# A second feed-forward product in seven block products, with the norms shared between VectorE and GpSimd

## The chip, the cores and the metric

One core of one Trainium2 chip runs the whole program. The metric is the device time in microseconds (us): the median of three timed runs is 3547.95 us, the runs lie between 3546.67 and 3548.14 us. All numbers of the trace come from one profiled execution, which took 3548.3 us; its recorded span, from the first to the last instruction, is 3546.4 us.

## The reference

Two layers work on 1056 tokens (1024 of a prompt, 32 of a sample group) of 1024 features. Only the second half of a layer matters here:

```python
x = layer_norm(ALPHA * x + mix @ w_out, ln1_g, ln1_b)
h = square(relu(x @ w_ff_up))                    # 1024 -> 4096 features
x = layer_norm(ALPHA * x + h @ w_ff_down, ln2_g, ln2_b)   # 4096 -> 1024

def layer_norm(x, g, b):
    mu = mean(x); var = mean(square(x - mu))
    return (x - mu) * rsqrt(var + 1e-5) * g + b
```

Ahead of it stand the input product, sliding-window attention and an RWKV-7 recurrence. All values are float32.

## The kernel before

**Layout.** Features lie on the 128 partitions, tokens in the columns. The tokens form three chunks: 0 and 1 of 384 columns, 2 of 288. A float32 product is made of three matmuls: each operand is split into a high part (a cast on ScalarE, L287 for data, L236 for weights) and the remainder as a low part (a subtraction on VectorE, L288 and L237), and high x high, high x low and low x high are summed in a PSUM bank (`gemm_parts`, `products`, `mmul` L206). A weight tile is 128 x 1024 (512 KB, loaded at L223), a block of features 128 x 384 (192 KB) or 128 x 288.

**Feed-forward, first product (`ff`).** The first four feature tiles are made chunk by chunk (`up`). The other 28 go by pairs (`pair_up`): for chunks 0 and 1, seven products stand in for the eight of a 2 x 2 block product; chunk 2 is done directly. Each result is passed through relu (ScalarE), squared (mostly on GpSimd, L1367) and stored in `d_h` in device memory, one transfer per tile and chunk.

**Second product.** 32 feature tiles are taken in eight groups of four. `features(g)` loads the 12 blocks of the next group (L1461) and splits them while the present group is multiplied. For each of 8 output tiles and 3 chunks, `down` sums 12 matmuls in one PSUM bank, and VectorE adds the bank to an accumulator in SBUF (L1472). The accumulators start as the residual, loaded from `d_x` (L1507).

**Norms.** `layer_norm` takes the mean from a product with ones, subtracts it (VectorE, L339), squares (ScalarE, L341), sums the squares (VectorE and GpSimd, L348), forms the reciprocal root by a Newton iteration on tiny tiles (VectorE, L298 to L302, L357), spreads it with a matmul, multiplies (L364), adds the bias and splits (ScalarE L369, VectorE L370). It is a generator in three parts: `book` puts these at given TensorE times (`LN_TIMES`, `LN1_TIMES`) among the matmuls that follow, and the order on TensorE is as written. In the last group the second product runs chunk by chunk, so chunks 0 and 1 are normed among the matmuls of the next chunk; chunk 2 comes last by itself. The other engines' order is set by a list scheduler; each engine, and SyncE's DMA queue, works strictly in its order.

**Buffers.** Blocks and splits live in slots (`Slots`): 16 "outer" ones per chunk (`x`), 20 "inner" ones per chunk (`i`), handed out and given back in program order.

## Time and profile before

| | |
|---|---|
| median of the runs | 3547.95 us |
| profiled execution, its span | 3548.3 us, 3546.4 us |
| TensorE busy | 3425.7 us, 97% |
| VectorE, ScalarE, GpSimd busy | 61%, 33%, 22% |
| chain that ended last | TensorE 83%, VectorE 6%, DMA 2% |
| granted TensorE clock, mean | 0.978 |

In layer 0 the branch products and the first norm end near 1062 us, the pairs of the first product run from about 1100 to 1385 us, the second product from there to about 1720 us, and layer 1 begins among its last norm. The second layer's second product ends at 3516 us, and the last chunk's norm follows alone. Busy time of an engine is an average over stages; what a stage waits for is in the view of waits, and what engines and DMA do in a stretch is in the table of windows.

### The profile page before, as it was taken

To read this page: it belongs to the slowest core of one execution; us is meant where nothing else is said; L and a number is where in the kernel's file an instruction comes from. 1 tells how busy PE (TensorE), PEld (TensorE's weight loads), DVE (VectorE), ACT (ScalarE), POOL (GpSimd) and SP (SyncE) were. 2 spreads that over 40 slices of the span, in tenths; PEclk is the share of its full clock that TensorE was granted. 3 is DMA by queue.
4 is the path that set the end of the run, shared out by engine and by line. 5 is a ranking of instruction groups with operands and counts; after the bars stand their busy time and mean duration, and the time that the engine had idled before them with its cause. 6 is when DMAs were issued, how large, how long until landed. Compare 5 with 4: busy or idle time off the path is not lost.

```text
span 3546.4 us, 65145 instructions
## 1 busy us (share of the span) xinstructions
PE 3425.7 (97%) x24950; PEld 3174.9 (90%) x24950; DVE 2153.1 (61%) x5492; ACT 1174.6 (33%) x2653; POOL 790.9 (22%) x1134
## 2 busy tenths in 40 slices
PE   8999999998989999999999999999999899999997
PEld 8688888888979999999897888888899799999997
DVE  4746778756476555444657467778473855554445
ACT  4654322222153333221237443222221533331112
POOL 2223423211122331000232234232101322310002
PEclk9999999999989999999999999999999999999998
DMA  5123323326213336232031333232251233362211
GB/s 169 62 87 115 86 77 85 83 67 202 66 64 118 110 99 197 93 97 77 13 89 49 100 102 91 79 84 82 100 176 48 90 111 110 107 197 87 90 47 50
DMA packets 282359, 342.08 MB, mean 96 GB/s; under 512 B 111168, under 2 KB 244832, under 8 KB 282016
## 3 DMA queue, kind: packets, MB, share of 16 engines
q1 hardware_dynamic: 253152, 297.84, 28.0%
q10 hardware_dynamic: 27360, 35.57, 2.8%
q8 instruction: 196, 3.21, 0.4%
q0 software_dynamic: 1536, 4.52, 0.3%
q14 instruction: 115, 0.94, 0.1%
HBM read 232.24 MB, written 102.21 MB: 94 GB/s over the span
## 4 chain that ended last, share of the span: by engine, by line
PE 83%; DVE 6%; DMA 2%; issue 1%; ACT 1%; POOL 1%; SPq 0%; ACTq 0%; DVEq 0%; POOLq 0%
PE mm L206 35%; PE b L206 25%; PE c L206 21%; PE b L210 1%; PE c L210 0%; PE b L793 0%; DVE pd L1019 0%; DVE i L364 0%; DVE x L1294 0%; DVE x L370 0%; DMA i<-d_x 0%; DMA x<-d_h 0%; DVE Xt L1021 0%; DMA i<-d_yr 0%; DMA d_g<-gs 0%
## 5 line engine op out<-in xcount | busy, mean ns | idle before, releaser
L206 PE MATMUL mm<-x,w 128*128 128x384 f32 (+1 forms) x6630 | 1320.9, 335 | 17.6 <-ACT x L287 8.5
L206 PEld LDWEIGHTS mm<-x,w 128*128 128x128 f32 x6630 | 1077.6, 190 | 72.5 <-issue 12.5
L236 ACT CAST w<-raw 128x1024 fp32r<-128x1024 f32 x260 | 273.0, 1050 | 568.1 <-PE b L206 364.3
L206 PE MATMUL b<-x,w 128*128 128x384 f32 (+1 forms) x1958 | 457.4, 320 | 0.8 <-DVE x L288 0.8
L206 PE MATMUL mm<-i,w 128*128 128x384 f32 (+1 forms) x2034 | 421.5, 328 | 19.0 <-ACT i L287 14.4
L237 DVE TENSOR_TENSOR w<-raw,w 128x1024 fp32r<-128x1024 f32 x260 | 321.4, 1236 | 176.6 <-ACT w L236 176.0
L206 PE MATMUL c<-i,w 128*128 128x384 f32 (+1 forms) x2080 | 426.8, 326 | 1.2 <-DVE i L1309 1.2
L206 PE MATMUL b<-i,w 128*128 128x384 f32 (+1 forms) x1570 | 391.6, 324 | 5.4 <-ACT i L287 5.4
L206 PEld LDWEIGHTS mm<-i,w 128*128 128x128 f32 x2034 | 347.3, 192 | 21.4 <-ACT i L287 14.6
L206 PEld LDWEIGHTS c<-i,w 128*128 128x128 f32 x2080 | 353.9, 191 | 3.7 <-DVE i L1309 1.8
L206 PEld LDWEIGHTS b<-x,w 128*128 128x128 f32 x1958 | 334.2, 188 | 1.5 <-DVE x L288 1.5
L206 PE MATMUL c<-x,w 128*128 128x384 f32 (+1 forms) x1424 | 311.9, 323 | 0.0
L206 PEld LDWEIGHTS b<-i,w 128*128 128x128 f32 x1570 | 276.4, 188 | 6.0 <-ACT i L287 6.0
L206 PEld LDWEIGHTS c<-x,w 128*128 128x128 f32 x1424 | 242.4, 190 | 0.5 <-DVE x L288 0.5
L1367 POOL TENSOR_TENSOR x<-x 128x384 f32<-128x384 f32 x112 | 114.5, 1023 | 365.2 <-ACT x L1366 319.9
L313 POOL TENSOR_TENSOR i<-i,i 128x384 f32<-128x384 f32 (+1 forms) x36 | 34.7, 963 | 686.3 <-DVE i L1472 680.1
L1472 DVE TENSOR_TENSOR i<-i,b 128x384 f32<-128x384 f32 x144 | 74.8, 520 | 144.2 <-PE b L206 143.7
L821 POOL TENSOR_TENSOR z<-z,gs 128x384 f32<-128x384 f32 (+1 forms) x84 | 80.2, 954 | 287.0 <-issue 184.4
L1366 ACT ACTIVATE x<-x 128x384 f32<-128x384 f32 x112 | 58.6, 523 | 246.1 <-DVE x L1434 153.6
L1100 POOL COPY sav<-vt 64x128 f32<-64x128 f32 x128 | 42.7, 334 | 331.6 <-PE c L206 300.2
L1127 DVE COPY sav<-c 64x128 f32<-64x128 f32 x128 | 36.9, 288 | 126.2 <-PE c L206 125.2
L287 ACT CAST x<-x 128x384 fp32r<-128x384 f32 (+1 forms) x126 | 60.5, 497 | 152.2 <-DMA x<-d_h 108.4
(349 smaller groups left out, 4974.2 us busy)
## 6 DMA issues: line engine op xcount, KB each, us to landing
raw<-in_w_in_dram SPq DMA_DIRECT2D x72, 512.0 KB
raw<-in_w_up_dram SPq DMA_DIRECT2D x64, 512.0 KB
raw<-in_w_down_dram SPq DMA_DIRECT2D x64, 512.0 KB
x<-d_h SPq DMA_DIRECT2D x128, 192.0 KB
d_h<-x SPq DMA_DIRECT2D x112, 192.0 KB
d_g<-gs ACTq DMA_DIRECT2D x64, 192.0 KB
i<-d_g SPq DMA_DIRECT2D x64, 192.0 KB
d_z<-z ACTq DMA_DIRECT2D x52, 192.0 KB
```

The source lines that it names most:

```text
L206: return self.nc.tensor.matmul(out, lhsT=lhsT, rhs=rhs, start=start, stop=stop)
L210: self.nc.tensor.transpose(out, x, ident)
L236: nc.scalar.copy(wf[:, 0, :], raw)
L237: self.weng.tensor_tensor(wf[:, 1, :], raw, wf[:, 0, :].bitcast(F32), op=ALU.subtract)
L287: self.nc.scalar.copy(hi, src)
L313: eng.tensor_tensor(sums[c].f, a, acc[k][c].f, op=ALU.add)
L821: nc.gpsimd.tensor_tensor(out[:, :n], out[:, :n], prev[:, :n], op=ALU.add)
L1100: nc.gpsimd.tensor_copy(sav[Kk, :], vt[Kk, k // 2, :])
L1127: nc.vector.tensor_copy(sav[B, :], sa[B, 0:128])
L1366: nc.scalar.activation(out=z.f, in_=z.f, func=AF.Relu)
L1367: P(z.f, z.f, z.f, op=ALU.mult)
L1472: nc.vector.tensor_tensor(a, a, p[:, :n], op=ALU.add)
```

## The change

The second product becomes seven block products over all 32 feature tiles, in the order 1, 2, 5, 4, 6, 7, 3. Feature tiles are taken in pairs and chunks 0 and 1 as the two column halves of a 2 x 2 block product. Each product has 8 jobs, and a job has one weight tile and two 128 x 384 blocks: 24 matmuls into four banks, which are kept over all 8 jobs. In products 1, 2, 5 and 4 a job also carries 24 matmuls on two 128 x 288 blocks of chunk 2, which is done directly. The combinations of squared features are formed once, in the first product: `quad` makes three more differences on GpSimd and one on VectorE per pair and stores seven blocks (`d_t`), `third` makes one for chunk 2 and stores three (`d_c`). The combinations of weights are made on GpSimd job by job (`weights`): one 128 x 1024 sum or difference per job in products 5, 6, 7 and 3. Blocks are now streamed: `prepare` loads and splits those of the job after next. What lands in the banks goes to the outputs in `done`, with a running sum per chunk for the norm (`total`).

In the norms, two of eight subtractions, three of eight multiplications and the three low parts behind them, and three of six sums of squares are on GpSimd; PSUM is copied by ScalarE first for these. The second norm's order is chunk 2 (booked at product 6), chunk 0 (at product 3), chunk 1 last; the next layer's attention takes the chunks in the order 0, 2, 1. The accumulators of chunks 0 and 1 share one set of 20 inner slots.

```diff
         sq = []
+        ms = get()
+        nc.scalar.copy(ms.f, pm[:, :n])
         for k in range(KD):
-            nc.vector.tensor_tensor(a[k], a[k], pm[:, :n], op=ALU.subtract)
+            if k in (1, 3):
+                nc.gpsimd.tensor_tensor(a[k], a[k], ms.f, op=ALU.subtract)
+            else:
+                nc.vector.tensor_tensor(a[k], a[k], pm[:, :n], op=ALU.subtract)
...
             else:
-                eng = (nc.vector, nc.gpsimd)[k % 2]
+                eng = nc.gpsimd if k < 5 else nc.vector
...
             self.mmul(pr[:, o:o + m], lhsT=rb[:, bi, :], rhs=self.ident[:, o - b:o - b + m], start=True, stop=True)
+        rs = get()
+        nc.scalar.copy(rs.f, pr[:, :n])
         for k in range(KD):
-            nc.vector.scalar_tensor_tensor(a[k], a[k], par[:, gcol + k:gcol + k + 1], pr[:, :n],
-                                           op0=ALU.mult, op1=ALU.mult)
-            bk = par[:, bcol + k:bcol + k + 1]
+            bk, gk = par[:, bcol + k:bcol + k + 1], par[:, gcol + k:gcol + k + 1]
+            pool = k in (1, 3, 5)
+            if pool:
+                nc.gpsimd.tensor_tensor(a[k], a[k], rs.f, op=ALU.mult)
+            else:
+                nc.vector.scalar_tensor_tensor(a[k], a[k], gk, pr[:, :n], op0=ALU.mult, op1=ALU.mult)
+            scale = gk if pool else 1.0
             if out is None:
                 hi, lo = [(self.outer if self.outer.free[c] else tmp).get(c, F32R) for _ in range(2)]
-                nc.scalar.activation(out=hi.t, in_=a[k], func=AF.Identity, bias=bk)
-                nc.vector.scalar_tensor_tensor(lo.t, a[k], bk, hi.f, op0=ALU.add, op1=ALU.subtract)
+                nc.scalar.activation(out=hi.t, in_=a[k], func=AF.Identity, bias=bk, scale=scale)
+                if pool:
+                    nc.scalar.activation(out=a[k], in_=a[k], func=AF.Identity, bias=bk, scale=scale)
+                    nc.gpsimd.tensor_tensor(lo.t, a[k], hi.f, op=ALU.subtract)
+                else:
+                    nc.vector.scalar_tensor_tensor(lo.t, a[k], bk, hi.f, op0=ALU.add, op1=ALU.subtract)
                 if keep is None:
                     acc[k].put()
...
+        def quad(k, b11, b12, b21, b22):
+            t1, t2, t4 = [get(0, F32) for _ in range(3)]
+            P(t1.f, b12.f, b11.f, op=ALU.subtract)
+            V(b12.f, b22.f, b12.f, op=ALU.subtract)
+            P(t2.f, b22.f, t1.f, op=ALU.subtract)
+            P(t4.f, t2.f, b21.f, op=ALU.subtract)
+            for t, z in ((1, b11), (5, t1), (7, b12), (3, b22), (6, t2), (2, b21), (4, t4)):
+                store(d_t[t - 1, k], z)
+        def third(k, x1, x2):
+            xd = get(2, F32)
+            P(xd.f, x2.f, x1.f, op=ALU.subtract)
+            for t, z in enumerate((x1, x2, xd)):
+                store(d_c[t, k], z)
...
+    def ff_down(self, l, inner, small, keep):
+        nc, tc, i = self.nc, self.tc, self.i
+        d_x, d_t, d_c = self.d_x[l], self.d_t[l], self.d_c[l]
+        V, P, S = nc.vector.tensor_tensor, nc.gpsimd.tensor_tensor, nc.vector.scalar_tensor_tensor
+        n, n2 = CH[0][1], CH[2][1]
+        acc = [[None] * 3 for _ in range(KD)]
+        sums = [Fixed(keep.tile([128, CH[c][1]], F32, tag=f"sum{c}", name=self.nm("sum"))) for c in range(3)]
+        sk = {}
+        def weights(p, k):
+            raw = lambda q: self.wraw(i["w_down"][l, q, k])
+            if p in (1, 2, 4):
+                return self.wsplit(raw({1: 0, 2: 1, 4: 3}[p]))
+            if p == 5:
+                a, b = raw(2), raw(3)
+                sk[k] = keep.tile([128, 1024], F32, tag=f"s{k}", name=self.nm("sk"))
+                P(sk[k], a, b, op=ALU.add)
+                return self.wsplit(sk[k])
+            if p == 6:
+                P(sk[k], sk[k], raw(0), op=ALU.subtract)
+                return self.wsplit(sk[k])
+            a = raw(3 if p == 7 else 1)
+            P(a, a, sk[k], op=ALU.subtract)
+            return self.wsplit(a)
+        def block(src, c):
+            z = self.outer.get(c)
+            nc.sync.dma_start(out=z.f, in_=src)
+            return self.parts(z, lambda: self.outer.get(c, F32R))
+        def prepare(p, k):
+            x = [block(d_t[p - 1, 2 * k + q], 1) for q in range(2)]
+            t = {1: 0, 2: 1, 5: 0, 4: 2}.get(p)
+            y = [block(d_c[t, 2 * k + q], 2) for q in range(2)] if t is not None else []
+            return weights(p, k), x, y
+        def residual(m, c):
+            acc[m][c] = inner.get(c)
+            nc.sync.dma_start(out=acc[m][c].f, in_=d_x[m, :, CH[c][0]:CH[c][0] + CH[c][1]])
+        def add(e, x, sign=1.0):
+            S(e, e, sign * ALPHA, x, op0=ALU.mult, op1=ALU.add)
+        def total(c, m, first, eng):
+            if first:
+                nc.scalar.copy(sums[c].f, acc[m][c].f)
+            else:
+                eng.tensor_tensor(sums[c].f, sums[c].f, acc[m][c].f, op=ALU.add)
+        def done(p, mp, e, y):
+            m = 2 * mp
+            if p == 1:
+                u[mp] = self.outer.get(0)
+                nc.scalar.copy(u[mp].f, e)
+            elif p == 2:
+                add(acc[m][0].f, e)
+                add(acc[m][2].f, y)
+                P(acc[m][0].f, acc[m][0].f, u[mp].f, op=ALU.add)
+                total(0, m, mp == 0, nc.gpsimd)
+                total(2, m, mp == 0, nc.gpsimd)
+            elif p == 5:
+                add(acc[m][1].f, e)
+                add(acc[m + 1][1].f, e)
+            elif p == 4:
+                add(acc[m + 1][2].f, y)
+                total(2, m + 1, False, nc.vector)
+                add(acc[m + 1][0].f, e, -1.0)
+            elif p == 6:
+                V(u[mp].f, u[mp].f, e, op=ALU.add)
+                P(acc[m][1].f, acc[m][1].f, u[mp].f, op=ALU.add)
+            elif p == 7:
+                V(u[mp].f, u[mp].f, e, op=ALU.add)
+                V(acc[m + 1][0].f, u[mp].f, acc[m + 1][0].f, op=ALU.subtract)
+                total(0, m + 1, False, nc.vector)
+                P(acc[m + 1][1].f, acc[m + 1][1].f, u[mp].f, op=ALU.add)
+                total(1, m + 1, mp == 0, nc.gpsimd)
+                u[mp].put()
+            else:
+                V(acc[m][1].f, acc[m][1].f, e, op=ALU.add)
+                total(1, m, False, nc.vector)
...
+                ends = dict(start=(k == 0 and q == 0), stop=(k == 7 and q == 1))
+                for t, z, nn, ends in ((e, x, n, ends), (y, xc, n2, dict(
+                        start=(p in (1, 5) and k == 0 and q == 0), stop=(p in (2, 4) and k == 7 and q == 1)))):
+                    for mp in range(4 if z else 0):
+                        hi, lo = z[q]
+                        for j, (a, b) in enumerate(((0, hi), (0, lo), (1, hi))):
+                            self.mmul(t[mp][:, :nn], lhsT=w[:, a, 4 * q + mp, :], rhs=b.t, start=ends["start"] and j == 0,
+                                      stop=ends["stop"] and j == 2)
+                            self.due(self.pe_ns)
...
+                if q + 2 < len(jobs):
+                    ready.append(prepare(*jobs[q + 2]))
+                if k == 0:
+                    if p in (1, 5):
+                        y = fours()
+                    e = fours() if p in (6, 3) else [self.ps(self.pb, "b") for _ in range(4)]
+                if (p, k) == (6, 0):
+                    self.book(norm(2), LN2_TIMES)
+                elif (p, k) == (3, 0):
+                    self.book(norm(0), LN2_TIMES)
+                if k == 3:
+                    for mp in range(4):
+                        for m, c in {2: ((0, 0), (0, 2)), 5: ((0, 1), (1, 1)), 4: ((1, 0), (1, 2))}.get(p, ()):
+                            residual(2 * mp + m, c)
+                w, x, xc = ready.popleft()
+                product(p, k, e, y, w, x, xc)
+                for t in x + xc:
+                    for z in t:
+                        z.put()
+                if k == 7:
+                    for mp in range(4):
+                        done(p, mp, e[mp][:, :n], y[mp][:, :n2])
             self.due()
...
```

**SyncE's queue in the second product.** `raw` is a weight load, `x0`/`x1` a block of 384 columns, `x2` one of 288; the digits behind are the slot and two running numbers, and the brackets name what the row waits for. Before, in the third and fourth group:

```order
L1461 DMA x0_13_2916_16300<-d_h0_104 128x384 [waits PE_49]
L1461 DMA x0_1_2990_16740<-d_h0_104 128x384 [waits DMAHW5_49,DVE_49]
L1461 DMA x0_7_2972_16704<-d_h0_104 128x384 [waits DMAHW6_49,DMAHW2_49,DVE_49]
L1461 DMA x0_4_2919_16306<-d_h0_104 128x384 [waits DMAHW7_49,PE_49]
L1461 DMA x2_6_2931_16330<-d_h0_104 128x288 [waits DMAHW0_49,PE_49]
L1461 DMA x2_1_2934_16336<-d_h0_104 128x288 [waits DMAHW1_49,PE_49]
L1461 DMA x0_13_2975_16710<-d_h0_104 128x384 [waits DMAHW4_49,DVE_49]
```

After, in products 6 and 7 of layer 0:

```order
L1572 DMA x1_11_3432_18844<-d_t0_104 128x384 [waits DMAHW6_49,DMAHW4_49,DVE_49]
L1572 DMA x1_5_3437_18880<-d_t0_104 128x384 [waits PE_49]
L240 DMA raw_3505_19163<-in_w_down_dram 128x1024 [waits DMAHW0_49,DVE_49]
L1572 DMA x1_11_3440_18886<-d_t0_104 128x384 [waits DMAHW6_49,DMAHW1_49,DVE_49]
L1572 DMA x1_1_3463_18971<-d_t0_104 128x384 [waits PE_49]
L240 DMA raw_3513_19205<-in_w_down_dram 128x1024 [waits DMAHW3_49,DVE_49,Pool_49]
L1572 DMA x1_11_3466_18977<-d_t0_104 128x384 [waits DMAHW1_49,DVE_49]
L1572 DMA x1_9_3471_19013<-d_t0_104 128x384 [waits DMAHW5_49,PE_49]
L1572 DMA x1_14_3479_19063<-d_t0_104 128x384 [waits PE_49]
```

Before, the group's blocks go through many slots. Now two blocks come per job, and every second one is put into the same slot, `x1_11`, whose row waits for VectorE (the split of the block that lay there); the other waits for TensorE.

**GpSimd in the second product.** Before, nothing stood there between the last squares of the first product and the sums of the norm:

```order
L1367 TENSOR_TENSOR x0_2_2765_15625<-x0_2_2765_15625 128x384 [waits Activation_49]
L1446 TENSOR_TENSOR x2_5_2772_15718<-x2_5_2772_15718 128x288 [waits DMAHW3_49,Activation_49,Pool_49]
L313 TENSOR_TENSOR i0_0_2_3319_18888<-i0_0_8_2773_15722,i0_0_0_2776_15725 128x384 [waits DVE_49]
L313 TENSOR_TENSOR i0_0_2_3319_18888<-i0_0_2_3319_18888,i0_0_1_2779_15728 128x384 [waits DVE_49,Pool_49]
L313 TENSOR_TENSOR i0_0_2_3319_18888<-i0_0_2_3319_18888,i0_0_12_2782_15731 128x384 [waits DVE_49,Pool_49]
```

After, around the end of product 6 in layer 0 (L1567 is a weight difference, L393 and L402 the norm of chunk 2, L1616 a sum of outputs):

```order
L393 TENSOR_TENSOR i0_2_13_3331_18257<-i0_2_13_3331_18257,i0_2_4_3446_18912 128x288
L402 TENSOR_TENSOR x2_3_3450_18921<-i0_2_6_3327_18249,x2_14_3449_18920 128x288 [waits DMAHW5_49,DMAHW4_49,Activation_49]
L1567 TENSOR_TENSOR raw_3513_19205<-raw_3513_19205,sk_3196_17590 128x1024 [waits DMAHW3_49,DVE_49]
L402 TENSOR_TENSOR x2_9_3454_18932<-i0_2_10_3329_18253,x2_15_3453_18931 128x288 [waits PE_49,Activation_49]
L402 TENSOR_TENSOR x2_5_3458_18943<-i0_2_13_3331_18257,x2_1_3457_18942 128x288 [waits PE_49,Activation_49]
L1616 TENSOR_TENSOR i0_0_16_3198_17595<-i0_0_16_3198_17595,x0_15_2994_16639 128x384 [waits DVE_49]
L1616 TENSOR_TENSOR i0_0_14_3200_17599<-i0_0_14_3200_17599,x0_7_2995_16641 128x384 [waits DVE_49]
L1616 TENSOR_TENSOR i0_0_17_3202_17603<-i0_0_17_3202_17603,x0_8_2996_16643 128x384 [waits DVE_49]
L1616 TENSOR_TENSOR i0_0_5_3204_17607<-i0_0_5_3204_17607,x0_9_2997_16645 128x384 [waits DVE_49]
L1567 TENSOR_TENSOR raw_3521_19247<-raw_3521_19247,sk_3220_17687 128x1024 [waits DMAHW0_49,Activation_49]
L1567 TENSOR_TENSOR raw_3529_19289<-raw_3529_19289,sk_3236_17768 128x1024 [waits DMAHW3_49,DVE_49,Activation_49]
L1567 TENSOR_TENSOR raw_3537_19331<-raw_3537_19331,sk_3108_17157 128x1024 [waits DMAHW6_49,DVE_49]
```

The row holds weight differences of 128 x 1024 between the steps of the norm and the sums of outputs; in products 7 and 3 they follow one another.

## Rows read from the trace of the kernel before

**Rows 1.** The page: span, busy time by engine, 40 slices of TensorE and its clock.

```profile
span 3546.4 us, 65145 instructions
...
PE 3425.7 (97%) x24950; PEld 3174.9 (90%) x24950; DVE 2153.1 (61%) x5492; ACT 1174.6 (33%) x2653; POOL 790.9 (22%) x1134
...
PE   8999999998989999999999999999999899999997
...
PEclk9999999999989999999999999999999999999998
```

**Rows 2.** Timeline of TensorE in the second product: start, length, instruction.

```profile
1650.69 0.30 PE L206 MATMUL b<-i,w 128*128 128x288 f32 x1
...
1652.28 0.34 PE L206 MATMUL mm<-x,w 128*128 128x384 f32 x1
...
1654.37 0.33 PE L206 MATMUL b<-x,w 128*128 128x384 f32 x1
```

**Rows 3.** Windows: stretch, its length, busy time by engine, clock, DMA share, GB/s.

```profile
1110.00:1360.00 250.00, 250.00 (x1575) 250.00 (x1574) 130.96 (x177) 81.56 (x132) 75.38 (x72) 1.00 0.34 108
1360.00:1410.00 50.00, 47.12 (x286) 46.18 (x284) 28.92 (x53) 21.59 (x43) 6.87 (x8) 0.97 0.82 261
1410.00:1700.00 290.00, 290.00 (x1817) 290.00 (x1816) 136.22 (x242) 56.72 (x91) 0.00 (x0) 1.00 0.28 86
...
1388.00:1392.00 4.00, 3.83 (x13) 3.31 (x13) 2.98 (x7) 1.59 (x4) 0.14 (x1) 0.57 0.93 296
```

**Rows 4.** Timeline of all engines: block loads and what splits them.

```profile
1567.06 4.86 SPq L1461 DMA_DIRECT2D x<-d_h  x6
...
1569.39 0.51 ACT L287 CAST x<-x 128x384 fp32r<-128x384 f32 x1 [7.91 <-DMA x<-d_h]
1569.94 0.56 DVE L288 TENSOR_TENSOR i<-x,x 128x384 fp32r<-128x384 f32 x1 [1.11 <-ACT x L287]
...
1375.53 3.81 SPq L1461 DMA_DIRECT2D x<-d_h  x7
1380.00 0.51 ACT L287 CAST x<-x 128x384 fp32r<-128x384 f32 x1 [8.94 <-DMA x<-d_h]
```

**Rows 5.** Timeline of VectorE and GpSimd beside each other, 78 to 136 us.

```profile
78.13 5.69 POOL L487 TENSOR_TENSOR qh<-qraw,qh 64x1024 fp32r<-64x1024 f32 x2 [0.63 <-ACT qh L486]
...
79.31 2.28 DVE L237 TENSOR_TENSOR w<-raw,w 128x1024 fp32r<-128x1024 f32 x1
81.51 2.34 DVE L468 TENSOR_SCALAR m<-m 128x2 f32<-128x2 f32 x1
...
86.16 0.16 DVE L468 TENSOR_SCALAR m<-m 128x2 f32<-128x2 f32 x1
...
86.50 1.22 DVE L237 TENSOR_TENSOR w<-raw,w 128x1024 fp32r<-128x1024 f32 x1
...
132.84 2.33 POOL L487 TENSOR_TENSOR qh<-qraw,qh 64x1024 fp32r<-64x1024 f32 x1
```

**Rows 6.** One line's instructions (L313): duration ns minimum/median/maximum over the span.

```profile
L313 POOL TENSOR_TENSOR i<-i,x x36: 803/1014/1108, 936.1 to 2774.9; 128x384 f32<-128x384 f32 x24, 128x288 f32<-128x288 f32 x12
```

**Rows 7.** TensorE's waits, 975 to 1062 us: waited for, total, times, longest.

```profile
PE b L206 <- DVE ln_rb L357: 9.8, 2, 7.4
PE b L206 <- DVE i L313: 5.3, 1, 5.3
```

**Rows 8.** TensorE's waits, 1360 to 1700 us.

```profile
PE b L206 <- ACT i L287: 2.6, 1, 2.6
```

**Rows 9.** TensorE's waits, 1700 to 1800 us.

```profile
PE b L206 <- DVE i L313: 5.1, 1, 5.1
PE b L206 <- DVE ln_rb L357: 2.4, 2, 1.3
```

**Rows 10.** Timeline of the end of the program.

```profile
3518.27 0.72 PE L206 MATMUL b<-i,ones 128*128 128x288 f32 x2
...
3539.14 3.57 ACT L376 ACTIVATE i<-i,par 128x288 f32<-128x288 f32 x8 [13.12 <-DVE i L364]
```

More of the change, by code (lines that the diff above doesn't have):

```diff
@@ L97, in put, with __init__ @@
         self.pool.free[self.c].append(self.j)
+class Fixed:
+    def __init__(self, t):
+        self.f = t
+    def put(self):
+        pass
 class Step:
@@ L416, in attention @@
             nc.gpsimd.memset(qs.rearrange("p a b c d -> p (a b c d)"), 0.0)
+            order = (0, 1, 2) if l == 0 else (0, 2, 1)
             def rope(zt, w, scale, dst=None):
@@ L420, in rope @@
                 rot = ap2.tile([128, T], F32, tag="qrot", name=self.nm("qrot"))
-                for ci, (c0, n) in enumerate(CH):
+                for ci in order if zt in (Z_AK, Z_Q) else range(3):
+                    c0, n = CH[ci]
                     p = yield from self.gemm_parts(w, 0, self.xr(ci), n)
@@ L535, in attention @@
             gk, gq = keys(), queries(0)
-            for ci in range(3):
+            for ci in order:
                 for _ in range(3 * KD + 1):
@@ L1442, in pair_up @@
                     release(B[t])
[L1443 to L1448 removed]
+            quad(f // 2, z, u, v, x)
         def release(pairs):
@@ L1453, in release @@
                     t.put()
[L1455 to L1472 removed]
+        zs = {}
         B = {t: [] for t in (1, 2, 3, 4)}
@@ L1482, in ff @@
                 if c == 1:
+                    for k in range(2):
+                        quad(k, *(zs[2 * k + q, e] for q in range(2) for e in range(2)))
                     tokens_up()
+            for k in range(2):
+                third(k, zs[2 * k, 2], zs[2 * k + 1, 2])
             self.due()
@@ new lines, in ff_down @@
+        u = {}
+        jobs = [(p, k) for p in (1, 2, 5, 4, 6, 7, 3) for k in range(8)]
+        ready = deque(prepare(*q) for q in jobs[:2])
+        fours = lambda: [self.ps(*b) for b in ((self.mm, "mm"), (self.mm, "mm"), (self.pc, "c"), (self.pc, "c"))]
+        with tc.manual_schedule(engines={mybir.EngineType.PE}):
+            for q, (p, k) in enumerate(jobs):
+                if q + 2 < len(jobs):
[20 more added lines that the diff above has]
+                        done(p, mp, e[mp][:, :n], y[mp][:, :n2])
@@ L1539, in ff @@
             self.early = {z: self.wload(i["w_in"][l + 1, z]) for z in (Z_AK, Z_AV, Z_Q)}
-        drain(norm(2, last=True))
+        drain(norm(1, last=True))
     def run(self):
@@ L1559, in run @@
                 self.gbanks = deque([(self.mm, "mm"), (self.pc, "c")])
-                self.ff(l, inner, sp, *self.mix(l, inner, sp))
+                self.ff_up(l, inner, sp, upper("wu"), *self.mix(l, inner, sp))
+                first.close()
+                assert len(inner.free[0]) == len(inner.free[1]) == 20
+                inner.share(0, 1)
+                self.ff_down(l, inner, sp, pool("sk"))
             self.wpools = deque([self.wp])
```

121 lines of the change are left out of this document (44 added, 77 removed).

## The prediction

> **What bounds the kernel now.** Start with the page: TensorE is busy 3425.7 of 3546.4 us, and the slices show 8 or 9 tenths nearly everywhere, at a clock of 9 in all slices but one [rows 1]. The windows then show which stages have room for nothing else: in the pairs and in the second product TensorE is busy throughout, while VectorE has about half of its time free and GpSimd does nothing in the second product [rows 3]. So there a matmul less is time less, as long as its inputs keep coming. The waits come last: they lie at the first norm, 9.8 and 5.3 us [rows 7], at the start of the second product, 2.6 us [rows 8], and at the change of layer, 5.1 and 2.4 us [rows 9]; the program ends with a norm that nothing covers [rows 10].
>
> **The matmuls removed.** Twelve matmuls of 384 columns take 1654.37 - 1652.28 = 2.09 us, 0.174 us each; twelve of 288 take 1.59 us, 0.1325 each [rows 2]. Before, a layer's second product has 8 groups x 8 tiles x 2 chunks x 12 = 1536 of 384 columns; after, 7 products x 8 jobs x 24 = 1344. Chunk 2 keeps its 768. That is 192 fewer per layer: 33.4 us, **-66.8 us** for both. These lie on the path, since nothing is waited for in that stretch but the 2.6 us at its start [rows 3, 8]; I leave those 2.6 us as they are (0 to 6 after).
>
> **The stream that takes their place.** A job with chunk 2 lasts 24 x (0.174 + 0.1325) = 7.36 us, one without 4.18 us. The 24 jobs of products 6, 7 and 3 (100 us per layer) are the tight ones. Each needs 512 + 2 x 192 KB = 917 kB, which in 4.18 us is 219 GB/s; DMA has done 261 GB/s at a share of 0.82 [rows 3], so bandwidth is there. What is short is the slot. Every second block goes through one slot: issue, landing, cast, low part, and only then the next issue. At 86 GB/s the cast started 1569.39 - 1567.06 = 2.33 us after the issue; with the queues at 261 GB/s it was 1380.00 - 1375.53 = 4.47 us. From cast to subtraction are 0.55 us, the subtraction takes 0.56 [rows 4]. The loop is thus 3.44 us at best and 5.58 at worst, and a job can't be shorter than the loop. Between the two by GB/s: at a period of 4.75 us the demand is 193 GB/s, 0.61 of the way from 86 to 261, so 2.33 + 0.61 x 2.14 + 1.11 = 4.75 us. That costs 24 x 0.57 = 13.7 us, less about one job of lead (4.2): 9.5 us per layer.
>
> The Trainium skill has a rule for this, in "DMA: Bandwidth & Descriptors", on the anatomy of one DMA: a transfer costs a fixed 2 us plus its bytes at 436 GB/s, by which 192 KB are an estimated 2.45 us at any load. By it the loop would be 3.56 us, no job would wait, and the time would be that of the first rival below; the light row agrees with it and the loaded row doesn't, so I go by the rows.
>
> **GpSimd beside VectorE.** The subtraction in that loop has a new neighbour. At 78.13 us GpSimd started two operations on 1024 columns, of which one alone takes 2.33 us; a weight subtraction of VectorE that began at 79.31 took 2.28 us and not 1.22, and ended at 81.59, 1.13 us after the first GpSimd operation was due to end. The second GpSimd operation then ran on until 83.82, and a VectorE instruction on two columns took 2.34 us and not 0.16 [rows 5]. The two engines take turns whole instructions at a time. In products 6, 7 and 3 GpSimd now has, per layer, 12 weight differences (the first four of product 7 stand ahead of the norm's rows in its order) x 2.33 = 28 us, and for outputs and two norms 22 operations of 1.01 us and 11 of 0.80 [rows 6]: 31 us, 59 us in all. A split that comes at a random moment waits on average (28 x 1.17 + 31 x 0.47) / 114 = 0.4 us (half an operation, over a stretch of 24 x 4.75 us). On 24 loops that is 10 us. With the 9.5 above I take **+20 us per layer, +40 us**. The bounds: nothing, if the loop is 3.44 us; 5.58 + 0.6 = 6.18 us at the other end, 24 x 2.0 - 4 = 44 us per layer, 88 us.
>
> The whole sum of turns gives a check. VectorE: 24 x (1.13 + 2 x 0.56) = 54 us of splits and 24 x 0.56 = 13 us of norms and sums; GpSimd: 59; together 126 us against 100, less two jobs of lead (4.5) and the last steps of chunk 0's norm that may come later (8.9): 13 us too much per layer. It falls on the same jobs as the 20 and is not added.
>
> The Trainium skill states this as a rule, in "SBUF — State Buffer", on who interferes with whom: a VectorE instruction with two inputs in SBUF and a GpSimd instruction that reads SBUF exclude each other for a whole instruction, and whichever starts second waits. By that rule alone, with transfers never late, the sum would be 3548.3 - 66.8 - 6 - 5 + 5 + 26 = 3501.5 us; the rows bear the rule out.
>
> **The norms.** At the first norm TensorE waits about 15.1 us per layer, for the Newton tiles and for the last sum [rows 7]. Eight VectorE instructions of some 0.5 us leave VectorE's queue in each norm, but GpSimd does them in 1.01 us [rows 6], and they take turns with VectorE's. VectorE now also waits for sums that GpSimd forms in its own order; behind such a wait stand the adds of the next chunk and the splits. I bound it at -9 and +6 us per layer and take -3: **-6 us**. At the change of layer 7.5 us of waits stood [rows 9]; now two of the three norms are done inside the products and the third is covered by the next layer's matmuls of chunk 0. Bounds -7.5 and +10; I take **-5 us**. The end of the program is the norm of chunk 1, 384 columns and not 288, from the product with ones at 3518.27 to the end at 3546.4, 28 us [rows 10]. Sixteen instructions in a row get longer by about 0.09 us, 1.4; three of the eight multiplications and two subtractions go to GpSimd at twice the time, and the outputs pass through three free slots, each held until its store is done: **+5 us** (-1 to +10).
>
> **The first product.** A pair gets three GpSimd operations of 1.01 us and one of 0.80 more per 20.9 us (twelve pairs take 250 us), which raises GpSimd from 75.4 of 250 us to about 0.48 of the time, and 0.56 us on VectorE (131 of 250) [rows 3, 6]. Stores grow from 960 KB to 1.78 MB per pair, some 40 GB/s on top of 108. All of this lies beside full TensorE work, and I cost it at nothing; if that cover fails, one turn of 1.0 us per pair would be 28 us.
>
> **The sum.** 3548.3 - 66.8 + 40 - 6 - 5 + 5 = 3515.5 us for an execution like the profiled one; the median of the runs is 0.35 us lower, so **3515 us**. With the stream between 10 and 30 us per layer this case spans 3491 to 3541.
>
> **Rivals.**
> - *The stream stays hidden* (chance 0.28). The loop is under 4.18 us because loads are spread evenly and land in 2.3 to 3.0 us. For it: a mean share of 0.28 in the second product before [rows 3]. Against it: the demand of these jobs is two and a half times as high. Then 3548.3 - 66.8 - 6 - 5 + 5 = 3475 us.
> - *The slot sets the pace, and the change is slower* (0.15, with the next). Landing at 4.47 us as in the loaded row, and a turn of GpSimd in most loops: 6.18 us per job. 3548.3 - 66.8 + 88 + 5 = 3574 us, with no gain at the norms. It decides from a loop of 5.9 us on: 24 x 1.7 - 4.2 = 36.4 us per layer, which eats 66.8 + 6. For it: each issue in SyncE's order also stands behind one that waits for TensorE, so a late block delays the next. Against it: at such a pace the demand falls to 150 GB/s, and landing gets quicker.
> - *The clock* (0.04 of that 0.15). After the wait of 2.6 us the granted clock was 0.57, near the lower level of 1.2 GHz, in 1388 to 1392 [rows 3, 8]. If the waits of single jobs kept it there, a job would take 8.4 us, and half of the 48 jobs so would cost 100 us: about 3580 us. Against it: three of the four slices with TensorE at 8 tenths still show a clock of 9 [rows 1].
> - *No difference* (0.10): a loop near 5.7 us and no gain at the norms, 3540 to 3555 us.
>
> **Chances and range.** My forecast's own case has 0.47. Within 0.2% is about 7 us, 3541 to 3555, what a measurement of this kernel can't tell from no change: 0.09. Slower: 0.15. Faster: 0.28 + 0.47 + 0.01 = 0.76. The range takes in the hidden stream and goes up to near the point where the slot eats the gain: 3466 to 3560.
>
> **What would show it.** Matmuls of the second product fewer by 384; in products 1, 2, 5 and 4 no waits of TensorE; in products 6, 7 and 3 waits for the low parts of the second block (VectorE) of 0.5 to 1 us a job, and blocks that land 3 to 4 us after issue; VectorE's 0.56 us subtractions stretched beside GpSimd. The forecast is wrong high if these 24 jobs run at 4.2 us, wrong low if they run at 6, or if the waits at the first norm grow beyond 15 us a layer.

## The result: slower by 35 us

The changed kernel takes 3583.1 us (median of four runs, 3575.3 to 3590.7) and the kernel before 3548.1 (3546.7 to 3550.7): 1.0087 of it, 95% interval 1.0059 to 1.0115. Forecast were 3515 us, 3466 to 3560. The page of the profiled execution (3590.65 us), against [rows 1]:

```profile
span 3588.9 us, 65576 instructions
...
PE 3402.8 (95%) x24566; PEld 3141.3 (88%) x24566; DVE 2244.7 (63%) x5335; ACT 1316.9 (37%) x2932; POOL 1196.8 (33%) x1419
```

TensorE has 384 matmuls less and is busy 22.9 us less, not 66.8; VectorE has 157 instructions less and is busy 91.6 us *more*. The marks of each stage in the two traces (first product with ones, first pair, first and last matmul of the second product, end) put the 42.5 us of span here: up to the first norm -2.0; the first norms +4.3 and +5.1; the pairs +2.6 and +2.5; the second product -1.3 (layer 0) and +9.7 (layer 1), where -33.4 each had been due for the matmuls alone; change of layer with the attention behind it +18.9; the end +2.7.

TensorE's waits over the whole span (waited for; total us, times, longest), first in the kernel before and then in the changed one:

```profile
PE b L206 <- DVE ln_rb L357: 27.6, 9, 7.4
PE b L206 <- DVE i L313: 16.3, 4, 5.3
...
PE mm L206 <- ACT qraw L423: 3.6, 2, 2.9
```

```profile
PE b L223 <- DVE ln_rb L381: 31.4, 3, 14.3
PE b L223 <- DVE sum L1593: 25.2, 4, 13.3
...
PE b L223 <- DVE i L1586: 14.3, 2, 7.9
PE mm L223 <- ACT qraw L462: 11.9, 3, 8.3
PE b L223 <- DVE x L305: 9.9, 7, 2.2
```

`sum` and `i L1586` (the evacuation, that is the add that empties a bank) are new: both stand where one product gives way to the next, not at the blocks inside products. The timeline of all engines at the change from the second to the third product of layer 0 (start, length, engine, line; in brackets the idle time before and what ended it) shows how the second comes about:

```profile
1508.74 0.33 SPq L1572 DMA_DIRECT2D x<-d_t  x1
1509.13 2.40 POOL L1561 TENSOR_TENSOR sk<-raw,raw 128x1024 f32<-128x1024 f32 x1 [4.35 <-DMA raw<-in_w_down_dram]
...
1509.87 2.35 DVE L305 TENSOR_TENSOR x<-x,x 128x288 fp32r<-128x288 f32 x2 [1.15 <-ACT x L304]
...
1512.25 0.33 SPq L1572 DMA_DIRECT2D x<-d_c  x1
...
1513.15 0.39 SPq L1572 DMA_DIRECT2D x<-d_t  x1
...
1516.81 0.51 ACT L304 CAST x<-x 128x384 fp32r<-128x384 f32 x1 [3.79 <-DMA x<-d_t]
1517.35 1.45 DVE L305 TENSOR_TENSOR x<-x,x 128x384 fp32r<-128x384 f32 x3 [3.53 <-ACT x L304]
...
1518.72 1.94 DVE L1586 SCALAR_TENSOR_TENSOR i<-i,b 128x384 f32<-128x384 f32 x4
...
1519.41 1.97 POOL L1604 TENSOR_TENSOR i<-i,x 128x384 f32<-128x384 f32 x2 [7.88 <-DVE i L1586]
1519.41 1.94 PE L223 MATMUL b<-x,w 128*128 128x384 f32 x5 [6.35 <-DVE i L1586]
```

Read it from the top. GpSimd starts a weight sum at 1509.13. Two splits of VectorE that begin at 1509.87 take 2.35 us (0.82 without a neighbour, below), until 1512.22; GpSimd's instruction ends at 1511.53. At 1512.25 SyncE issues again: it had waited for the slot that these splits give back, and the block behind it in the same queue leaves only at 1513.15. Its data are there 3.66 us later. VectorE, which executes in order, idles 3.53 us in front of that block's split, and the evacuation behind it, whose data were complete at 1513, starts at 1518.72. TensorE waits 6.35 us and then runs at the lower clock (granted 0.50 from 1519 to 1524; 12 matmuls in 3.98 us instead of 2.09). This one turn passes on its own 1.5 us. The rest of the lateness was there before it: each block waits for a slot, then for its landing, and earlier turns stand in that loop too (two splits at 1498.13 take 2.12 us, 1.03 without the weight sums).

At the change to the last product GpSimd's and VectorE's instructions alternate in front of the norm of chunk 0:

```profile
1718.00 1.20 PE L223 MATMUL mm<-x,w 128*128 128x384 f32 x6
...
1724.02 1.01 DVE L1618 TENSOR_TENSOR x<-x,b 128x384 f32<-128x384 f32 x2
...
1728.14 2.66 POOL L1567 TENSOR_TENSOR raw<-raw,sk 128x1024 f32<-128x1024 f32 x1
...
1728.52 0.54 DVE L1618 TENSOR_TENSOR x<-x,b 128x384 f32<-128x384 f32 x1
1728.99 2.23 DVE L1593 TENSOR_TENSOR sum<-sum,i 128x384 f32<-128x384 f32 x1
...
1736.21 0.54 DVE L1593 TENSOR_TENSOR sum<-sum,i 128x384 f32<-128x384 f32 x1
...
1736.81 1.65 PE L223 MATMUL b<-sum,ones 128*128 128x384 f32 x2 [13.26 <-DVE sum L1593]
```

The same operation, L1593, takes 0.54 us free and 2.23 beside a weight difference; L1618, which reads one of its operands from PSUM, keeps its 0.54 there. From the end of product 7 (1718.0) to the last sum are 18.75 us, and the product with ones, written 5 us into the last product, holds up everything behind it on TensorE.

### The profile page after: what moved, and what is told of

It is laid out like the page before. It is cut to its first block, busy times and chain, and to the rows that moved or that the text cites. A ratio compares the mean times of both kernels' runs of the same rounds, so it can differ in the third digit from the quotient of the medians.

```text
span 3588.9 us, 65576 instructions
## 1 busy us (share of the span) xinstructions
PE 3402.8 (95%) x24566; PEld 3141.3 (88%) x24566; DVE 2244.7 (63%) x5335; ACT 1316.9 (37%) x2932; POOL 1196.8 (33%) x1419
## 4 chain that ended last, share of the span: by engine, by line
PE 75%; DVE 7%; DMA 4%; issue 3%; ACT 2%; POOL 2%; SPq 1%; ACTq 0%; DVEq 0%; POOLq 0%
PE mm L223 33%; PE b L223 21%; PE c L223 19%; DMA x<-d_t 2%; PE b L227 1%; DVE x L305 1%; DMA x<-d_c 1%; DVE w L254 1%; PE b L832 1%; PE c L227 0%; ACT x L304 0%; DMA i<-d_ya 0%; DVE i L371 0%; DVE pd L1058 0%; DVE x L404 0%
## 5 line engine op out<-in xcount | busy, mean ns | idle before, releaser
L223 PE MATMUL b<-x,w 128*128 128x384 f32 (+1 forms) x2662 | 519.5, 336 | 32.9 <-DVE i L1586 14.3
L223 PEld LDWEIGHTS b<-x,w 128*128 128x128 f32 x2662 | 462.2, 191 | 38.1 <-issue 14.7
L223 PE MATMUL c<-x,w 128*128 128x288 f32 (+1 forms) x1988 | 366.0, 318 | 0.0
L305 DVE TENSOR_TENSOR x<-x,x 128x384 fp32r<-128x384 f32 (+1 forms) x382 | 256.8, 708 | 169.8 <-ACT x L304 160.1
L304 ACT CAST x<-x 128x384 fp32r<-128x384 f32 (+1 forms) x390 | 177.1, 483 | 355.8 <-DMA x<-d_t 236.1
L223 PE MATMUL mm<-i,w 128*128 128x384 f32 (+1 forms) x1366 | 259.6, 333 | 17.6 <-ACT i L304 16.2
L223 PE MATMUL c<-i,w 128*128 128x384 f32 (+1 forms) x1372 | 254.1, 329 | 0.0
L223 PEld LDWEIGHTS mm<-i,w 128*128 128x128 f32 x1366 | 231.9, 192 | 22.0 <-ACT i L304 16.8
L223 PEld LDWEIGHTS c<-i,w 128*128 128x128 f32 x1372 | 230.4, 190 | 0.3
L223 PE MATMUL b<-i,w 128*128 128x384 f32 (+1 forms) x770 | 158.7, 330 | 0.0
L223 PEld LDWEIGHTS b<-i,w 128*128 128x128 f32 x770 | 132.3, 188 | 0.0
```

The source lines that it names most:

```text
L223: return self.nc.tensor.matmul(out, lhsT=lhsT, rhs=rhs, start=start, stop=stop)
L304: self.nc.scalar.copy(hi, src)
L305: self.nc.vector.tensor_tensor(lo, src, hi.bitcast(F32), op=ALU.subtract)
```

## The experiments

The runs were made on four chips, each time with the kernel before beside them, so that kernels of different groups are compared by their ratios to it. Theory A at the outset: these evacuations and sums stand too far back in VectorE's order, the shared norms have longer chains, and TensorE is slowed by where the inner tiles lie. Rival B, from the prediction: the slots pace the products. As the runs came in, A's first part fell and was replaced by theory L: GpSimd's new work holds VectorE's up, and all the rest follows. Ratios come with their 95% intervals.

**The changed kernel again.** 

> The changed kernel as it is, so that the pieces below have a time of it on the same chip. Expected: 3575 to 3591 us, 1.0059 to 1.0115 of the kernel before, as in its first four runs; matmuls with an inner tile as moving operand at 0.1766 us for 384 columns, TensorE's longest waits in the second product of layer 0 at 6.35 us (change from second to third product) and 13.26 us (the mean of chunk 0).

 Measured: 3581.2 us, 1.0077 (1.0059 to 1.0095). In its trace TensorE waits 16.8 us in all for i L1586, 27.2 for sum and 11.6 for x L305; the totals below are held against these.

**Order on VectorE.** In the whole second product, then in products 1, 2, 5, 4 alone:

```
-        with tc.manual_schedule(engines={mybir.EngineType.PE}):
+        with tc.manual_schedule(engines={mybir.EngineType.PE, mybir.EngineType.DVE}):
...
-                if q + 2 < len(jobs):
+                if k < 7 and q + 2 < len(jobs):
                     ready.append(prepare(*jobs[q + 2]))
...
                         done(p, mp, e[mp][:, :n], y[mp][:, :n2])
+                    if q + 2 < len(jobs):
+                        ready.append(prepare(*jobs[q + 2]))
```

> In the second product VectorE's order is the written one, and of a product's last job the evacuations are written ahead of the splits of the block after next. Theory A (evacuations stand behind splits of blocks that land late): the wait for VectorE at the change from the second to the third product goes from 6.35 and 7.91 us to under 2, done(7)'s first sum starts within 1 us of the product's end and not 6 us after it, so the wait for sum falls from 13.26 and 9.12 by 5 to 6 us, and the half clock behind these waits shortens: -20 to -35 us. Rival B (the one slot per job sets the pace, whatever VectorE's order is): the waits move to x L305, time within 6 us of the changed kernel; the first job after each change may even be later by 3 to 4 us, since its blocks are fetched later.

Measured: 3621.1 us, 1.0192 (1.0167 to 1.0217), 40 us slower than without, which neither side expected. The wait at 1513 was gone and the total for sum fell to 2.8 us, as A wanted; but in products 7 and 3 (1690 to 1735, then 1735 to 1800 us) TensorE now waited for

```profile
PE b L223 <- DVE w L254: 3.5, 2, 3.2
PE mm L223 <- DVE w L254: 3.4, 1, 3.4
...
PE b L223 <- DVE i L371: 8.9, 2, 8.7
PE mm L223 <- DVE i L1625: 6.6, 1, 6.6
```

> The written order on VectorE with evacuations ahead of the splits after next, as in the run where the whole second product had it, but only in its first four products (1, 2, 5, 4); products 6, 7 and 3 with their norms keep the scheduler's order. There the waits at the change from the second to the third product fell from 6.8 to 1 us while waits for weights and for the norms' chains came in products 7 and 3. Theory A: here the first stays and the second does not come: waits for i L1586 under 4 us in both layers instead of 12.6 and 4.1, -8 to -18 us. Rival (VectorE's order only moves a wait to the next late operand): within 4 us of the changed kernel.

Measured: 3584.4 us, 1.0079 (1.0064 to 1.0095). The rival holds: the waits for i L1586 fell from 16.8 to 10.1 us, those for sum rose from 27.2 to 29.3, and the time stayed. So order alone is not the cause: what stands first in VectorE's order only decides who waits.

**Booking the norm later.**

```
-self.book(norm(0), LN2_TIMES)
+self.book(norm(0), [13000, 22000, 28000])
```

> The norm of chunk 0 is booked 8 us later: its mean's product 13 us into the seventh product, and not 5, the later parts at 22 and 28 us. Theory A1 (booked before its sum can be there): the wait for sum, 13 us and 9 to 10 us, goes to under 3 each, with the half clock behind it, and the end of that norm moves by less: -12 to -25 us. Theory A2 (the chain of that norm is the path to the next layer and to the end, wherever it is booked): the waits come back at ln_rb and at the first product of the next layer, within 6 us of the changed kernel.

Measured: 3591.2 us, 1.0094 (1.0071 to 1.0117). A1 falls: the waits for sum went (2.8 us left) and no time came off. A2 is right that the waits come back, but not where: those at ln_rb and qraw are unchanged, and they come as 18.3 us for x L305 in front of `mm` matmuls (2.8 without the edit; the longest, 9.4, at the start of the last product) and as 10.3 for i L371 (4.4 without).

**More slots for raw blocks.**

```
-z = self.outer.get(c)
+z = self.outer.get(0 if c == 1 else c)
```

> The raw blocks of the 384-token part come into slots of chunk 0, so that more of them can be in flight. Rival B, the prediction's stream term (one slot per job sets a pace of 4.75 us in products 6, 7 and 3): those products lose their waits on x L305 and the time falls by 15 to 40 us. Theory A: only the few x L305 waits (12.6 us over both layers, of which about half is queueing on VectorE) can go, -2 to -8 us, and the waits for i L1586 and sum stay at 13 and 25 us.

Measured: 3567.2 us, 1.0046 (1.0027 to 1.0065), 11 us by the ratios: between the two. The waits for x L305 fell to 2.7 us and those for i L1586 to 8.4, but sum rose to 36.2. What the slot does is seen in product 7, all of whose matmuls write `b`: in the changed kernel it runs from 1677.36 to 1718.00 (the line at 1718.00 above), here from 1681.54 without a gap.

```profile
1677.36 2.93 PE L223 MATMUL b<-x,w 128*128 128x384 f32 x16
```

```profile
1681.54 33.44 PE L223 MATMUL b<-x,w 128*128 128x384 f32 x192
```

Its eight jobs take 40.6 us (layer 0) and 45.7 (layer 1) in the changed kernel, 5.1 and 5.7 us a job, and 33.3 in both layers here, 4.2 a job. So in product 7 the slot does set the pace; but much of what it gives back is waited for again at sum. In product 6 it doesn't: 36 to 37 us in both kernels.

**Weight sums and differences on VectorE.** 64 operations of 128x1024, 32 per layer, in products 5, 6, 7 and 3. The lines show the edit for products 7 and 3; the two lines that write `sk[k]` are changed in the same way:

```
-            P(a, a, sk[k], op=ALU.subtract)
+            V(a, a, sk[k], op=ALU.subtract)
```

> The weight sums and differences of products 5, 6, 7 and 3 (32 of 128x1024 per layer) go from GpSimd to VectorE. If the turns between the two engines make the sums and splits late (part of theory A and of the prediction's stream term): VectorE's chain after the seventh product shortens from 12.7 towards 8 us and the waits in products 6, 7 and 3 fall by some 5 us a layer, -5 to -15 us. If VectorE's queue is what counts: 32 more operations of over 1 us in front of its splits, +5 to +20 us.

Measured: 3543.5 us, 0.9965 (0.9951 to 0.9980): 40 us less by the ratios, far more than either side expected. VectorE's groups by line (count | busy us, mean ns | idle before), first the changed kernel in 1640 to 1770 us, then this one in 1630 to 1755:

```profile
L305 DVE TENSOR_TENSOR x<-x,x 128x384 fp32r<-128x384 f32 x42 | 32.0, 780 | 13.5 <-ACT x L304 13.4
L254 DVE TENSOR_TENSOR w<-raw,w 128x1024 fp32r<-128x1024 f32 x17 | 28.0, 1650 | 5.4 <-ACT w L253 5.3
```

```profile
L305 DVE TENSOR_TENSOR x<-x,x 128x384 fp32r<-128x384 f32 x42 | 23.9, 590 | 4.3 <-ACT x L304 4.2
L254 DVE TENSOR_TENSOR w<-raw,w 128x1024 fp32r<-128x1024 f32 x18 | 23.5, 1312 | 5.5 <-ACT w L253 5.5
L1567 DVE TENSOR_TENSOR raw<-raw,sk 128x1024 f32<-128x1024 f32 x12 | 15.1, 1271 | 1.8 <-DMA raw<-in_w_down_dram 1.6
```

Splits went from 780 to 590 ns. VectorE took on 64 operations of 1.22 us, 78 us, and over the span it is busy 2230.1 us against 2244.7: its instructions had been longer by some 93 us beside GpSimd's weight sums. The gain lies in the second product, 39 to 43 us over both layers by the marks of this trace and the changed kernel's two, and product 7 takes 33.3 us in both layers. The chain at the change of products is gone too:

```profile
1506.06 0.82 DVE L305 TENSOR_TENSOR x<-x,x 128x288 fp32r<-128x288 f32 x2
...
1515.00 1.28 PE L223 MATMUL b<-x,w 128*128 128x384 f32 x6 [0.73 <-DVE i L1586]
...
1718.20 1.65 PE L223 MATMUL b<-sum,ones 128*128 128x384 f32 x2 [10.22 <-DVE sum L1593]
```

0.73 us instead of 6.35, with the evacuations still behind the splits in VectorE's order; over both layers i L1586 is down from 16.8 to 2.6 us. The wait for sum is only down from 13.26 to 10.22: GpSimd's other sums remain in that chain. The edit also makes each weight sum shorter (1.22 us for 2.40 to 2.65), so that SyncE gets the slots of raw weights back earlier: over both layers it waited 41.1 us for these sums in the changed kernel and 26.5 here. TensorE waits 0.5 us for split weights in the changed kernel, so little of the loss can have come that way directly, but no run separates it from the turns.

**The norms as before.** layer_norm is that of the kernel before, the rest as changed.

```
-                eng = nc.gpsimd if k < 5 else nc.vector
+                eng = (nc.vector, nc.gpsimd)[k % 2]
...
-            if pool:
-                nc.gpsimd.tensor_tensor(a[k], a[k], rs.f, op=ALU.mult)
```

> The norms' arithmetic goes back to the engines of the kernel before (mean, scale and residual split on VectorE and ScalarE), everything else is as changed. Theory A (sharing with GpSimd stretches the norms' chains): the first norm's longest wait for ln_rb goes from 14.2 back to about 7.4, the x L404 wait of 4.5 goes but the i L313 one of 5.3 returns, so -2 to -5 us per layer there; at the change of layer the 8.3 us wait for qraw returns to 3.6; the end of the program from 33.0 to about 30: together -10 to -25 us. Rival (the prediction's sign: sharing is worth 11 us by itself): +5 to +15 us. Rival D (nothing but the book of due times): within 4 us.

Measured: 3560.5 us, 1.0033 (1.0020 to 1.0047), 16 to 21 us less. And the other way round, the kernel before with the new norms alone:

> The kernel before with only the norms' new division between VectorE and GpSimd; its second product is the old one. The prediction had -11 us for that part (first norm -6, change of layer -5, end +5 once). Theory L: it is a loss by itself, +12 to +22 us over the kernel before: the first norm +4 to +5 per layer, change of layer +5, end +3 to +4. Rival (the division only costs beside the new second product): within 5 us of the kernel before.

Measured: 3565.5 us, 1.0036 (1.0020 to 1.0052): 13 us slower by the ratio, with the old second product. In its trace the first norms are 2.5 us longer each and the end 2.7, less than Theory L had; the longest wait for qraw is 2.9 us as in the kernel before, so the new norms don't make that one. TensorE's waits at the first norm of layer 0 in the changed kernel, with the old norms, and in the kernel before with the new ones:

```profile
PE b L223 <- DVE ln_rb L381: 14.2, 1, 14.2
PE mm L223 <- DVE x L404: 4.5, 1, 4.5
```

```profile
PE b L223 <- DVE ln_rb L374: 8.2, 2, 6.1
PE b L223 <- DVE i L330: 5.3, 1, 5.3
```

```profile
PE b L206 <- DVE ln_rb L364: 13.0, 1, 13.0
PE mm L206 <- DVE x L387: 4.5, 1, 4.5
```

18.7 us, 13.5, 17.5 (15.1 in the kernel before, [rows 7]): the new norms carry their wait with them. A part of why `ln_rb` is late stands in the changed kernel's timeline: the Newton steps on 128x3 elements take 0.15 us alone and 0.95 beside GpSimd.

```profile
1051.90 1.27 POOL L1441 TENSOR_TENSOR x<-x,i 128x384 f32<-128x384 f32 x1 [3.51 <-DVE ln L319]
...
1052.23 0.96 DVE L317 TENSOR_TENSOR ln<-ln 128x3 f32<-128x3 f32 x1
...
1053.13 4.08 POOL L1441 TENSOR_TENSOR x<-x,x 128x384 f32<-128x384 f32 x3
...
1053.58 0.95 DVE L318 SCALAR_TENSOR_TENSOR ln<-ln,ln_v 128x3 f32<-128x3 f32 x1
```

From the first of these steps to `ln_rb` are 14.3 us, and 8.4 with the old norms. Five stretched steps instead of two make 2.4 us of that; the rest is in VectorE's other instructions between the steps, some of them stretched too. GpSimd's L1441 belongs to the first product and has its like in the kernel before, so these rows show the price of a turn, not what the division alone adds.

What did not come true is the change of layer: the wait for qraw, 8.3 us in the changed kernel, is 8.7 with the old norms, and 8.3 to 8.7 in all changed kernels below.

**Both, and with the slots.**

> The two edits that took GpSimd off VectorE's port and gained by themselves, together: the weight sums and differences of the second product on VectorE (3543.5 us alone) and the norms as in the kernel before (3560.5 us alone, the changed kernel at 3581). Theory L (all of the loss is GpSimd's work beside VectorE's: the two losses stand in different places): the gains of 38 and 20 us add up, 3520 to 3528 us, which is the fastest so far; the first norm's longest wait back at 7.5 us and VectorE's busy time at about 2230 us or less. Rival (both gains are one chain, that of the seventh product to the norm of chunk 0): 3535 to 3545 us.

Measured: 3510.9 us, 0.9893 (0.9870 to 0.9915). Theory L: the gains add, and a little more. VectorE's busy time, 2253.2 us, did not come down to the 2230 that it had.

> As c3, with the 384-token raw blocks in slots of chunk 0 besides (alone that gave 3567 us against 3581). Theory L: the waits that the slots took away were those behind late weight loads, which the first edit has already taken, so within 5 us of c3. Rival B (the slots pace the products by themselves): another 10 to 14 us off, 3508 to 3515 us.

Measured: 3503.2 us, 0.9872 (0.9855 to 0.9889): 7.7 us off, between the two; the intervals overlap, so this step by itself is not shown.

**Where the inner tiles lie.** In the changed kernel matmuls that stream an inner tile run at 0.1766 us for 384 columns, in the kernel before at 0.1734, both at a granted clock of 1.00 (920 to 980 us). The allocation order of the changed kernel puts these tiles 32 bytes beyond a multiple of 512, that of the kernel before 448 beyond.

```
-v = small.tile([128, 3], F32, tag="ln_v", ...)
+v = small.tile([128, 16], F32, tag="ln_v", ...)[:, 0:3]
```

With 16 columns the inner tiles start 64 bytes beyond, with 112 columns (the second of these runs) 448.

> The small tile ln_v gets 16 columns instead of 3 and only 3 are used, so that the inner tiles behind it start at a multiple of 64 bytes (134720) as in the kernel before, and not 32 bytes beside one (134688). Order and engines of all work stay. Theory A (where the tile starts sets the pace): the 384-column matmuls on inner tiles go from 0.1766 to 0.1734 us and those of 288 columns from 0.1329 to 0.1322, some 3,500 of them, about -12 us, time 3565 to 3575. Rival C (pace differs by run or chip, or by what the neighbours read): pace stays at 0.1766, time within 3 us of the changed kernel run beside it.

> Placement again: ln_v takes 112 columns, so that the inner tiles start at 135104, which is 448 beyond a multiple of 512 bytes as the inner tiles of the kernel before and the outer ones of both, where the run with 134720 (64 beyond) had 0.1761 us for 384 columns instead of 0.1766. If the offset within 512 bytes sets the pace: 0.1734 us, some 3,500 matmuls by 3.2 ns, about -11 us. If not: 0.176 and within 3 us of the changed kernel, and the cause of this pace stays open.

Measured: 3584.8 us, 1.0083 (1.0060 to 1.0107), at 0.1760 us on average; and 3579.8 us, 1.0084 (1.0067 to 1.0101), at 0.1736. Place does set the pace; a start at a multiple of 64 isn't enough, and 448 is what restored it. TensorE's timeline, the changed kernel first (10 in 1.77 us), then the tiles at 448 (18 in 3.12):

```profile
934.80 1.93 PE L223 MATMUL mm<-i,w 128*128 128x384 f32 x10
936.57 3.35 PE L223 MATMUL c<-i,w 128*128 128x288 f32 x24
```

```profile
934.82 3.28 PE L223 MATMUL c<-i,w 128*128 128x384 f32 x18
937.94 3.28 PE L223 MATMUL mm<-i,w 128*128 128x384 f32 x18
```

The time of the whole program did not show it there. The pairs did, where TensorE is never idle: they are 2.6 and 2.5 us longer than before in the changed kernel, and 0.3 and 0.6 with the tiles at 448. So the same edit was put on the kernel whose waits were gone:

> The three edits together (3503.2 us) with the inner tiles 448 bytes beyond a multiple of 512, which in the changed kernel brought the 384-column matmuls on inner tiles back from 0.1766 to 0.1734 us while its time, 3579.8 against 3581.2 us, did not show it. If TensorE bounds those stretches now that the waits are gone: some 3,500 x 3.2 ns = 11 us less, 3490 to 3495 us. Rival (the time it saves is taken back at the next wait, as it was before): 3500 to 3506 us.

Measured: 3495.0 us, 0.9856 (0.9836 to 0.9876), 8.2 us below its like without it; TensorE's busy time fell by 13.0 us. By the ratios it is 6 us, and the intervals overlap, so for the whole program's time this step is likely and not shown; the pace and the time of the pairs are.

```profile
span 3488.4 us, 65493 instructions
...
PE 3359.9 (96%) x24566; PEld 3106.0 (89%) x24566; DVE 2254.7 (65%) x5486; ACT 1303.8 (37%) x2899; POOL 948.7 (27%) x1268
```

This version beats both kernels. Last, GpSimd out of the second product altogether (done()'s sums on VectorE too):

> As the one with the placement, and all that is left on GpSimd in the second product (16 sums with a half of the first two products, 20 or so running sums per layer) on VectorE as well. Theory L (what GpSimd does there, VectorE pays as well): no slower, -2 to -6 us, mostly at the wait for sum before the norm of chunk 0 (12.5 us in two layers with the three edits). Rival (these few are well placed, beside VectorE's idle time): +2 to +10 us, the chain to that norm longer.

Measured: 3499.4 us, 0.9858 (0.9838 to 0.9877): no difference. The waits for sum fell from 12.6 to 6.0 us, and those for the evacuations (L1567 there) rose from 2.2 to 9.0. The rest of GpSimd's work there was no part of the loss that these runs can see.

## Why the prediction was wrong

The profiled execution lies 75 us above the forecast for it: 35 in the second product, 24 at the change of layer with the attention behind it, 15 at the first norms, 5 in the pairs, and 4 the other way in the rest.

- *The matmuls removed, -66.8 us*: right. In the last version but one, with GpSimd's weight sums and norms taken back, more slots and the tiles at 448, TensorE is busy 3359.9 us, 65.8 less than in the kernel before. Its time is 51 to 53 us below, since changes of product still cost waits.
- *GpSimd beside VectorE*: the step that failed. The rows were read rightly ([rows 5]: whole instructions in turn), and the rule of the Trainium skill (SBUF — State Buffer, who interferes with whom) holds here, 0.54 us becoming 2.23. But the turns were counted on one instruction of 24 jobs, 0.4 us on average on a split in products 6, 7 and 3, 10 us a layer, and at nothing anywhere else. That mean was not too small: splits there took 0.78 us instead of 0.59. By the marks in the traces products 6, 7 and 3 together take 132.1 and 135.5 us in the two layers and 121.5 and 121.1 with the weight sums on VectorE: 11 and 14 us, near the 10. The same weight sums cost another 9 us a layer in products 1, 2, 5 and 4 (253.8 and 255.4 us against 244.7 and 246.9), so that the edit took 20 a layer off by the runs' times, and the norms another 8 to 10 where the forecast had a gain. Two things were missing. The count: 12 differences a layer, where 32 sums and differences a layer run beside the stream, product 5's among them, which are made while product 2 still runs (2.40 to 2.65 us each by the lines' means, not 2.33). And the turn was not passed on: split, slot, SyncE's queue, block, VectorE's queue, evacuation, TensorE, clock. The check by sums was for the tight jobs alone and was then not added.
- *Products 1, 2, 5 and 4 without waits*: wrong; 6.35 and 7.91 us stand at the change from the second to the third.
- *The stream, slot loop 4.75 us, +9.5 us a layer*: half right. In product 7, a third of the 24 jobs, the slot and the turns together set a pace of 5.1 and 5.7 us a job; more slots alone, or no weight sums alone, bring it to 4.2. Product 6 did not have it. More slots gave back 11 us for both layers (0 to 7.7 once the weight sums were gone); 19 had been put down. The landing time of 3.66 us lies between the two rows used. The 2.45 us that the prediction works out from the Trainium skill ("DMA: Bandwidth & Descriptors", anatomy of one DMA) is for transfers issued from GpSimd, as that section says; SyncE issues these blocks, and 3.66 us is what one took beside two weight loads. The rival in which all 24 jobs take 6.18 us is refuted; that its 3574 us came near the time is luck.
- *The norms, -6, -5 and +5 us*: the signs of the first two were wrong. The new division alone costs 13 us. "GpSimd does them in 1.01 us" is no gift if VectorE stands still meanwhile, least of all in a chain of eleven small steps.
- *The end, +5*: +2.7. *The first product, nothing*: +2.6 and +2.5, but that is the place of the inner tiles; at 448 bytes it is 0.2 and -0.1 with the same differences on GpSimd, so its cover held.
- *Clock rival*: not as a state that feeds itself, but behind the two long waits of layer 0 TensorE ran at a lower granted clock (0.50 in 1519 to 1524 us, 0.62 in 1736 to 1742).

Some of the prediction's figures are slips, and the forecast hangs on none of them. The clock reads 8 in two slices of [rows 1], not in one; a stream between 10 and 30 us per layer spans 3495 to 3535 us, not 3491 to 3541; a pair stored 4 x 192 + 2 x 144 = 1056 KB before, not 960.

Open stays the wait for qraw at the change of layer. It is 7.9 us or more in every kernel with the new second product and 2.9 in the two with the old one, so it comes with the second product or with the new order of chunks behind it (that order was not tried back). It accounts for 5.4 of the +18.9 us. The rest can't be told from one trace: the stretch up to the first norm, which no experiment's edit touches, lies between -9.3 and +8.2 us in these traces, and the change of layer with its attention between +2.5 and +24.2 in those of the changed kernel and its variants. In 2060 to 2260 us of the changed kernel the granted clock was 0.93 to 0.97, and 1.00 in the kernel before, without a wait to explain it.

## What to carry to other kernels

Before giving GpSimd work "on an idle engine", look whether VectorE is busy with two SBUF inputs in that stretch: then VectorE pays too. Here 163 us of weight sums on GpSimd made VectorE's own instructions some 93 us longer, more than the 78 us that it takes to form these sums itself. A delay on an in-order engine is priced by following who queues behind it (slot, DMA queue, evacuation), not by its mean length; product changes, where an accumulator must be emptied, are where it comes due. Moving the booking or the order of late work moved the wait in these runs, and only taking away what made it late took time off.

## What the runs showed of the hardware that was not expected

A matmul's pace changed with the place of its tiles in SBUF: with the streamed operand 32 bytes beyond a multiple of 512, 384 columns took 0.1766 us, 64 beyond 0.1760 and 448 beyond 0.1734 to 0.1736, at a granted clock of 1.00. Only these three places were tried, and whether the weights' place plays a part was not separated.
